# Experts' weights laid down by partition and loaded by 2 MB, in a ring of nine 16-KB tiles

## The chip, the cores and the metric

The program runs on one core of a Trainium2 chip. The metric is the device time of one execution in microseconds. Three executions of the kernel before were timed: 2105.32, 2105.45 and 2109.12 us, median 2105.45 us.

## What is computed

Three blocks follow each other on one sequence of 256 tokens with 1024 features, all in float32. The change lies in the first block's mixture of experts, cut here to what matters:

```python
probs = softmax(h2 @ w_router + b_router)
vals, idx = lax.top_k(swapaxes(probs, 1, 2), cap)      # 16 experts, each takes 32 tokens
for each expert e:
    xe = h2[idx[e]]                                    # [32, 1024]
    ye = (silu(xe @ w_gate_e[e]) * (xe @ w_up_e[e])) @ w_down_e[e]
    out[idx[e]] += vals[e] * ye
```

`w_gate_e` and `w_up_e` are [16, 1024, 2048], `w_down_e` is [16, 2048, 1024]: 8 MB for each of an expert's three matrices, 24 MB for an expert, 384 MB in all (MB is 1,048,576 bytes where loads are counted). Each weight is used once, for 32 tokens.

## The kernel before

`body` (L1667) runs `block1`, `moe`, `block2`, and twice `mixers` and `ffn`. All weights come in by `Net.load` (L71), on SP's queue, in the order in which they are written down. `Net.slot` (L79) hands out the tiles of a ring in turn; a tile is [128, 2048] floats, 8 KB per partition. `load_rows` (L85) cuts a weight into loads of up to 2048 columns per partition, 1 MB each. A row of the weight is a contiguous run in DRAM: a gate or up load is [128, 2048], one run of 8 KB per partition; a down load is [128, 2, 1024], two runs of 4 KB; a load of [128, 4, 512] has four runs of 2 KB.

The ring is six tiles (L41); in block 1 five more are added (L1673). `moe` goes on with these eleven, and puts the six row tiles of block 1's pool `ap8` in where they come free (L701): 17 tiles, 17 MB. From block 2 on it is the six tiles again (L1682). A load into a tile waits until the last reader of the tile's former content is done. SP also waits, at each load, for the landing of the load eight before it (the semaphores `DMAHW0` to `DMAHW7` in the order of the instructions), so at most eight are on their way.

In `moe` (L692) an expert's `gate` and `up` are eight loads each: per load eight matmul instructions of PE at L814, four column groups side by side. Then `hs = silu(gate) * up` on ACT and DVE (L827, L828), its transposes on PE (L831, L839), and eight loads of `down` with their matmuls at L857. The result is scaled on DVE (`Y`, L860) and scattered back to tokens by PE (L864). The first expert's matmuls stand between those that gather the chosen rows (`gather`, L756).

The last expert's `down` goes by two column halves (L846), in loads of [128, 4, 512]. Behind the first half, `out(0)` (L775) adds the result to `x`, transposes it into block 2's input and squares it; `next_load` (L795) brings the first weights of block 2 and splits them into two ring tiles, and `next_products` (L799) puts their products among the matmuls of the second half.

In block 1, 2 and 3 a projection takes each 1-MB load as pieces that ACT and DVE split in two (L99, L100) and PE multiplies three times (L147, L148, L149).

Of the kernel before, what the change touches and what calls it, by code (L numbers as in the profile page):

```python
# [9 lines left out]
F32 = mybir.dt.float32  # L10
# [16 lines left out]
RING_A8 = (6, 7, 8, 9, 12, 15)  # L27


def row_bc(src, n):  # L30
    """A [n] DRAM vector seen by all partitions."""
    return bass.AP(src.tensor, src.offset, [[0, P], [1, n]])


class Net:
    def __init__(self, ctx, tc, a, vo, out):
# [4 lines left out]
        self.rings = [(pool("wrp", 6), "wr")] * 6  # L41
        self.ring_at, self.last_load, self.last_mm = 0, None, None
# [21 lines left out]
    def hT(self, tag, dt=F32R):  # L64
        """One of the two [128, 8, 256] tiles that carry a phase's transposed input."""
        return self.hp.tile([P, 2048], dt, tag=tag, name=tag).rearrange("p (k t) -> p k t", t=S)
# [4 lines left out]
    def load(self, dst, src):  # L71
        """The loads on this queue go out in the order that they are written down in."""
# [6 lines left out]
    def slot(self, dt=F32):  # L79
        """The next tile of the loads' rings."""  # L80
        pool, tag = self.rings[self.ring_at % len(self.rings)]
        self.ring_at += 1
        return pool.tile([P, 2064 if tag == "a8" else 2048], dt, tag=tag, name="wr")

    def load_rows(self, src):  # L85
        """The rows of src [k * 128, n] as [128, k tiles, n], in loads of up to 2048 columns; yields (first k tile, view)."""
# [15 lines left out]
    def behind(self, ins):  # L102
        """The next weights that are split wait on DVE behind ins."""
        self.held = [ins] * 3

    def split_to(self, t, raw):
        """Weights split into the two halves of a tile."""
# [15 lines left out]
    def proj(self, xh, xl, loads, n, evac, ahead=0):  # L123
        """out[half][128, n] = sum over k; loads are (first k tile, raw view [128, k tiles, n]). The first half of the rows
        takes the last pieces, ahead in number, before the second one does."""
# [27 lines left out]
    def queued(self):  # L153
        """The products of this block go out behind the last one that was noted, whichever is ready first."""
# [3 lines left out]
    def table(self, func, after):  # L158
        """Has the activation function's table in place before the data is; after [128, 1] is the last user of another one."""
        self.nc.scalar.activation(self.cp.tile([P, 1], F32, tag="warm", name="warm"), after, func)  # L160

    # Side work goes between the pieces of the projections: generators, run a step at a time in order.
# [4 lines left out]
    def soon(self, f):  # L167
        """Ahead of the other side work: one such closure per step."""
# [8 lines left out]
    def step(self):  # L177
        """A step of the first task, and of the next ones while the steps are light."""
# [7 lines left out]
    def finish(self, gen=None):  # L186
        """Emits side work up to the end of gen, or all of it."""
# [5 lines left out]
    def proj_cols(self, xh, xl, w, c0, n, evac, ahead=0):  # L193
        """Column chunk [c0, c0 + n) of a weight."""
# [9 lines left out]
    def rstd(self, ms, n, d, name, pool=True):  # L204
        """(ms / d + eps) ** -0.5 on [128, n] sums of squares: a power on Pool, or Newton steps on DVE where Pool is busy."""
# [11 lines left out]
        # Newton steps r (3 - t r r) / 2, with the factors -1/2 put off to the end  # L217
# [7 lines left out]
    def sumsq(self, x, n, name, ss=None):  # L225
        """Sums of squares over the last axis of x [128, 2, n], into ss [128, 2]."""
# [7 lines left out]
    def transpose_to(self, src, kts, consume, k0=0):  # L234
        """src [128 tok, 2, kts * 128] -> consume(kt, n, bank [128, n, 256]) for pairs of kt from k0 on."""
# [29 lines left out]
    def input_T(self, gain, name):  # L265
        """The residual stream as the next phase's input: its rows' rstd, and x^T * gain split in two, by column
        halves as they come. The rows' rstd is applied to the products, not to x."""
# [12 lines left out]
class InputT:  # L280
# [6 lines left out]
    def columns(self, c, soon=False):  # L287
        """Column half c; soon: its transposes go between the next projection's pieces."""
# [18 lines left out]
def gate_row(N, dst, src, j0, off):  # L307
    """dst[p, :] = mod[off:off + 1024] for every p, from column tiles j0, j0 + 1 of src, plus b_ada."""
# [10 lines left out]
def block1(N, stop):  # L319
    nc, a, tc = N.nc, N.a, N.tc  # L320
    x = N.x
    with ExitStack() as ctx:
# [3 lines left out]
        p8 = ctx.enter_context(tc.tile_pool(name="ap81", bufs=1))  # L326
# [1465 lines left out]
```

## Time and profile before

| | |
|---|---|
| median of the runs | 2105.45 us |
| runs | 2105.32 to 2109.12 us |
| span of the profiled execution | 2108.0 us (first to last instruction) |
| PE busy | 1756.7 us, 83% |
| DVE / ACT / POOL busy | 819.4 / 603.7 / 181.9 us |
| moved by DMA | 616.02 MB, mean 292 GB/s |

The profile takes one execution apart; that execution's time outside the profiler isn't given, so its span, 2108.0 us, stands for it, 2.6 us above the median of the runs. The page cuts the span into 40 slices of 52.7 us: busy tenths of each engine, TensorE's granted clock in tenths, the busy share of the 16 DMA engines in tenths, and what they moved. The experts lie between about 264 and 1198 us, slices 6 to 22. The chain of waits follows the work that ended last back to the start.

### The profile page before, as it was taken

Reading aid. Unit: us, or ns where it says so; the run is one execution under the profiler, and the core shown is the slowest. Engines: PE = TensorE matmul, PEld = TensorE weight load, DVE = VectorE, ACT = ScalarE, POOL = GpSimd, SP = SyncE. Lnnn points to the kernel's source line nnn. Section 1 sums busy time; section 2 is a strip of 40 time slices with the busy share of each in tenths; the row PEclk is TensorE's granted clock in tenths of the full one; section 3 lists DMA queues with packets and bytes.
Section 4 is the critical chain, followed back from the end, with each engine's and each line's share of the span. In section 5 each row is a group of like instructions: output and inputs, shape, how many; then the busy total and the mean of one; then the engine's idle time right before and its main releaser. Section 6 shows DMA issues by size and latency. Waiting matters only on the chain.

```text
span 2108.0 us, 22814 instructions
## 1 busy us (share of the span) xinstructions
PE 1756.7 (83%) x8895; PEld 1002.8 (48%) x8895; DVE 819.4 (39%) x1563; ACT 603.7 (29%) x1074; POOL 181.9 (9%) x135
## 2 busy tenths in 40 slices
PE   7989786566666666666666899999999999999998
PEld 4767631110110111111100487777778888778886
DVE  4797610000000000000000356676775545786554
ACT  4545410000000000000000345445545445455443
POOL 0671100000000000000000131112010000110000
PEclk9999897877777777766777899999999999999999
DMA  9879699999999999999999773336325556516551
GB/s 363 351 287 348 242 386 422 422 423 422 421 424 424 421 422 423 422 423 420 424 424 423 281 275 120 130 124 210 123 94 183 180 180 207 162 52 198 193 171 70
DMA packets 174396, 616.02 MB, mean 292 GB/s; under 512 B 11336, under 2 KB 20744, under 8 KB 139216
## 3 DMA queue, kind: packets, MB, share of 16 engines
q1 hardware_dynamic: 170288, 601.21, 73.4%
q0 software_dynamic: 3568, 12.75, 1.9%
q8 instruction: 70, 1.15, 0.2%
q10 hardware_dynamic: 432, 0.60, 0.1%
q14 instruction: 38, 0.31, 0.0%
HBM read 613.45 MB, written 4.24 MB: 293 GB/s over the span
## 4 chain that ended last, share of the span: by engine, by line
PE 51%; DMA 41%; DVE 5%; ACT 1%; issue 1%; POOL 0%; POOLq 0%; SPq 0%; DVEq 0%; ACTq 0%
DMA wr<-w_gate_e_dram 14%; DMA wr<-w_up_e_dram 14%; PE pb L147 13%; PE pb L148 13%; PE pb L149 13%; DMA wr<-w_down_e_dram 13%; PE pb L814 2%; DVE wl L100 2%; PE pb L242 2%; PE pb L1360 2%; PE pb L1372 1%; PE po L1398 1%; PE pb L760 1%; PE pb L1056 0%; PE pb L1055 0%
## 5 line engine op out<-in xcount | busy, mean ns | idle before, releaser
L100 DVE TENSOR_TENSOR wl<-wr,wh 128x1024 fp32r<-128x1024 f32 (+1 forms) x380 | 416.3, 1106 | 259.5 <-ACT wh L99 258.8
L814 PE MATMUL pb<-wr,XT 128*32 128x512 f32 x2048 | 362.8, 801 | 183.2 <-DMA wr<-w_up_e_dram 108.6
L99 ACT CAST wh<-wr 128x1024 fp32r<-128x1024 f32 (+1 forms) x380 | 340.0, 897 | 337.0 <-PE pb L149 313.1
L147 PE MATMUL pb<-wh,hh 128*128 128x512 f32 (+3 forms) x992 | 392.2, 396 | 1.8 <-ACT wh L99 1.2
L148 PE MATMUL pb<-wl,hh 128*128 128x512 f32 (+3 forms) x992 | 379.7, 383 | 6.6 <-DVE wl L100 6.5
L149 PE MATMUL pb<-wh,hl 128*128 128x512 f32 (+3 forms) x992 | 379.3, 383 | 0.0
L814 PEld LDWEIGHTS pb<-wr,XT 128*32 128x32 f32 x2048 | 47.9, 122 | 480.7 <-DMA wr<-w_up_e_dram 273.9
L857 PE MATMUL pb<-wr,hT 128*32 128x512 f32 x1024 | 186.7, 807 | 90.4 <-DMA wr<-w_down_e_dram 82.9
L828 DVE TENSOR_TENSOR hs<-pb,hs 128x512 f32<-128x512 f32 x16 | 11.1, 692 | 573.7 <-PE pb L814 573.7
L147 PEld LDWEIGHTS pb<-wh,hh 128*128 128x128 f32 x992 | 189.7, 191 | 50.0 <-issue 12.7
L148 PEld LDWEIGHTS pb<-wl,hh 128*128 128x128 f32 x992 | 189.8, 191 | 43.4 <-DVE wl L100 11.3
L149 PEld LDWEIGHTS pb<-wh,hl 128*128 128x128 f32 x992 | 189.3, 191 | 34.7
L827 ACT ACTIVATE hs<-pb 128x512 f32<-128x512 f32 x16 | 9.6, 598 | 543.9 <-PE pb L814 543.9
L857 PEld LDWEIGHTS pb<-wr,hT 128*32 128x32 f32 x1024 | 30.4, 127 | 229.3 <-DMA wr<-w_down_e_dram 194.6
L860 DVE TENSOR_TENSOR Y<-pb,gfr 128x512 f32<-128x512 f32 (+1 forms) x17 | 11.8, 692 | 269.1 <-PE pb L857 269.1
L841 ACT COPY Sc<-pb 128x256 f32<-128x256 f32 x16 | 6.0, 373 | 324.8 <-PE pb L839 324.8
L788 POOL TENSOR_TENSOR x<-x,grow 128x512 f32<-128x512 f32 x4 | 5.1, 1285 | 913.0 <-ACT jk L231 913.0
L147 PE MATMUL pb<-wh,ah 128*128 128x512 f32 x176 | 69.9, 397 | 0.0
L148 PE MATMUL pb<-wl,ah 128*128 128x512 f32 x176 | 69.6, 395 | 0.0
L149 PE MATMUL pb<-wh,al 128*128 128x512 f32 x176 | 69.6, 395 | 0.0
L864 PE MATMUL acc<-Y,Sc 64*128 64x512 f32 x128 | 45.9, 813 | 15.3 <-DVE Y L860 15.3
L1353 ACT ACTIVATE sb<-sb,cm 128x256 f32<-128x256 f32 x64 | 32.1, 503 | 40.5 <-DVE cm L1350 40.5
(505 smaller groups left out, 1794.3 us busy)
## 6 DMA issues: line engine op xcount, KB each, us to landing
wr<-w_gate_e_dram SPq DMA_DIRECT2D x128, 1024.0 KB, 19.6
wr<-w_up_e_dram SPq DMA_DIRECT2D x128, 1024.0 KB, 19.7
wr<-w_down_e_dram SPq DMA_DIRECT2D x128, 1024.0 KB, 19.6
wr<-w_in_dram SPq DMA_DIRECT2D x62, 1024.0 KB, 7.9
wr<-w_ada_dram SPq DMA_DIRECT2D x24, 1024.0 KB, 12.2
wr<-w_gate_dram SPq DMA_DIRECT2D x22, 1024.0 KB, 5.1
wr<-w_up_dram SPq DMA_DIRECT2D x22, 1024.0 KB, 5.1
wr<-w_down_dram SPq DMA_DIRECT2D x20, 1024.0 KB, 5.0
```

Of the source, the lines that this page charges most:

```text
L99: self.nc.scalar.copy(hi, src)
L100: self.nc.vector.tensor_tensor(lo, src, hi.bitcast(F32), ALU.subtract)
L147: nc.tensor.matmul(o, xh[:, kt, tok], hv[:, k, :], start=kt == first, stop=False)
L148: nc.tensor.matmul(o, xh[:, kt, tok], lv[:, k, :], start=False, stop=False)
L149: self.last_mm = nc.tensor.matmul(o, xl[:, kt, tok], hv[:, k, :], start=False, stop=kt == last).ins
L242: self.nc.tensor.transpose(pv[:, j, h * P:(h + 1) * P], src[:, h, (k + j) * P:(k + j + 1) * P], self.ident)
L760: nc.tensor.matmul(pg, part[:, h, k * P:(k + 1) * P], G[:, h, es].rearrange("p e c -> p (e c)"), start=(h == 0 and i == 0), stop=(h == 1 a ...
L814: N.last_mm = nc.tensor.matmul(pacc[32 * j:32 * j + 32, :], XT[:, k + kk, e, :], wt[:, kk, j * 512:(j + 1) * 512], start=(k + kk == 0), st ...
L857: nc.tensor.matmul(py[32 * q:32 * q + 32, :], hT[:, b, 32 * j:32 * j + 32], wt[:, i, n * 512 - c0:n * 512 - c0 + 512], start=(j == 0 and b ...
L864: nc.tensor.matmul(acc[n][h], Sc[r, h * P:(h + 1) * P], Y[r, :], start=(e == 0), stop=(e == NE - 1))
L1353: nc.scalar.activation(sb[:, c], (ps if bias is None else sb)[:, c], AF.Exp, bias=mm[:, h:h + 1], accum_out=sm[:, h:h + 1])
L1360: nc.tensor.matmul(ps[:, h * S:(h + 1) * S], q[:, h * P:(h + 1) * P], k, start=True, stop=True, tile_position=tile_position)
```

## The change

- The three experts' weights are laid down on the host as [16 experts, 4 loads, 128, 4096]: `we_gate`, `we_up` and `we_down`. Each load is then one contiguous 2 MB in DRAM, with one run of 16 KB for each partition. The last expert's `we_down` is laid down by column halves.
- `load_packed` loads these into whole 16-KB tiles. Of the last expert's second half, the second 2 MB come as two loads of 1 MB.
- The ring's tiles are [128, 4096], 16 KB: three, three more in block 1, and three more in `moe` from a new pool `wx2`, which lies where `ap8` lay (`ap8` now ends with block 1). All other loads stay 1 MB and take the two halves of a tile one after the other; the tile comes free when both are used.
- The scratch for descriptors that POOL writes is 4 KB per partition (`SCRATCH`) and was 16 KB by default.
- `rxT`, the router's transposed rows, moves from `ap8` to the tile `b8`. Comments and docstrings are gone.

```diff
-RING_A8 = (6, 7, 8, 9, 12, 15)
+SCRATCH = 4096
...
-        self.rings = [(pool("wrp", 6), "wr")] * 6
-        self.ring_at, self.last_load, self.last_mm = 0, None, None
+        self.rings = [(pool("wrp", 3), "wr")] * 3
+        self.ring_at, self.rest, self.last_load, self.last_mm = 0, None, None, None
...
-    def slot(self, dt=F32):
-        """The next tile of the loads' rings."""
+    def slot(self, dt=F32, wide=False):
+        if self.rest is not None and not wide:
+            t, self.rest = self.rest, None
+            return t
         pool, tag = self.rings[self.ring_at % len(self.rings)]
         self.ring_at += 1
-        return pool.tile([P, 2064 if tag == "a8" else 2048], dt, tag=tag, name="wr")
+        t = pool.tile([P, 4096], dt, tag=tag, name="wr")
+        self.rest = None if wide else t[:, 2048:]
+        return t if wide else t[:, :2048]
+
+    def load_packed(self, src, n, narrow=()):
+        at = 0
+        for i in range(src.shape[0]):
+            for q in ((0, 2048), (2048, 4096)) if i in narrow else ((0, 4096),):
+                m = q[1] - q[0]
+                t = self.slot(wide=m == 4096)
+                self.load(t, src[i, :, q[0]:q[1]])
+                yield at, t.rearrange("p (a b) -> p a b", b=n)
+                at += m // n
...
-            self.xT = N.T("rxT", F32, 4)
+            self.xT = N.b8("rxT").rearrange("p h n -> p (h n)")[:, :1024].rearrange("p (k t) -> p k t", t=S)
...
+        wx2 = ctx.enter_context(tc.tile_pool(name="wx2", bufs=3))
...
-        for i in RING_A8:
-            N.rings.insert(i, (N.ap8, "a8"))
+        for i in (4, 5, 8):
+            N.rings.insert(i, (wx2, "wr"))
...
-            N.ahead += [(k, p, N.split_to(N.slot(F32R), p)) for k, p in N.pieces(raw, at)]
+            t = N.slot(F32R, wide=True)
+            N.ahead += [(k, p, N.split_to(t[:, 2048 * i:2048 * i + 2048], p)) for i, (k, p) in enumerate(N.pieces(raw, at))]
...
-            for w, pacc in ((a["w_gate_e"], psG), (a["w_up_e"], psU)):
+            for w, pacc in ((a["we_gate"], psG), (a["we_up"], psU)):
...
-                for k, wt in N.load_rows(w[0, e]):
+                for k, wt in N.load_packed(w[e], 2048):
...
-                for at, wt in N.load_rows(a["w_down_e"][0, e, :, c0:c0 + 512 * len(ns)]):
-                    if c0 and at == 4:
-                        next_products()
+                wd = a["we_down"][e]
+                for at, wt in N.load_packed(wd if len(ns) > 1 else wd[2 * ns[0]:2 * ns[0] + 2], 512 * len(ns), (1,) if c0 else ()):
                     for i in range(wt.shape[1]):
+                        if c0 and at + i == 4:
+                            next_products()
...
-        with tc.tile_pool(name="bm", bufs=1) as N.bm, tc.tile_pool(name="wx1", bufs=5) as wx, \
-                tc.tile_pool(name="ap8", bufs=6) as N.ap8:
-            N.rings = N.rings + [(wx, "wr")] * 5
+        N.rings0 = N.rings
+        with tc.tile_pool(name="bm", bufs=1) as N.bm, tc.tile_pool(name="wx1", bufs=3) as wx:
+            N.rings = N.rings + [(wx, "wr")] * 3
             N.router = Router(N)
-            block1(N, stop)
+            with tc.tile_pool(name="ap8", bufs=6) as N.ap8:
+                block1(N, stop)
...
-        N.rings, N.ring_at = [r for r in N.rings if r[0] not in (wx, N.ap8)], 0
+        N.rings, N.ring_at, N.rest = N.rings0, 0, None
...
+def experts(inputs):
+    r = {}
+    for n, name in (("we_gate", "w_gate_e"), ("we_up", "w_up_e")):
+        w = np.asarray(inputs[name])[0]
+        r[n] = np.ascontiguousarray(w.reshape(NE, 4, 2, P, 2048).transpose(0, 1, 3, 2, 4)).reshape(NE, 4, P, 4096)
+    w = np.asarray(inputs["w_down_e"])[0]
+    d = np.ascontiguousarray(w.reshape(NE, 4, 4, P, D).transpose(0, 1, 3, 2, 4)).reshape(NE, 4, P, 4096)
+    d[-1] = w[-1].reshape(2, 8, P, 2, 512).transpose(3, 0, 2, 1, 4).reshape(4, P, 4096)
+    r["we_down"] = d
+    return r
...
-    nc = bacc.Bacc("TRN2", target_bir_lowering=False, num_devices=1)
+    nc = bacc.Bacc("TRN2", target_bir_lowering=False, num_devices=1, dynamic_dma_scratch_size=SCRATCH)
```

What moves on the engines: the compute instructions of PE, DVE, ACT and POOL stay the same in number and, but for about a dozen that change places by a few at the start and at the end of the experts, in order. SP's loads of the experts become half as many and twice as large. At the last expert's three matrices and the loads behind them, SP's order before is (`wr` are tiles of the ring, `128x4x512` is partitions x runs x columns):

```order
L73 DMA wr<-w_gate_e_dram 128x2048 x8
L73 DMA wr<-w_up_e_dram 128x2048 x8
L73 DMA wr<-w_down_e_dram 128x4x512 x4
L73 DMA wr<-w_in_dram 128x4x512
L73 DMA wr<-w_down_e_dram 128x4x512 x4
L73 DMA wr<-w_in_dram 128x4x512
L73 DMA wr<-w_in_dram 128x4x280 x2
```

And in the changed kernel:

```order
L73 DMA wr<-we_gate_dram 128x4096 x4
L73 DMA wr<-we_up_dram 128x4096 x4
L73 DMA wr<-we_down_dram 128x4096 x2
L73 DMA wr<-w_in_dram 128x4x512
L73 DMA wr<-we_down_dram 128x4096
L73 DMA wr<-we_down_dram 128x2048 x2
L73 DMA wr<-w_in_dram 128x4x512
L73 DMA wr<-w_in_dram 128x4x280 x2
```

The bytes come in the same order; the first column half of `down`, four loads of 1 MB, is now two of 2 MB.

In block 2, where the ring is six halves, SP's order before has a wait for a tile at every load (`DMAHW` are the landings, `DVE` is the tile's last split):

```order
L73 DMA wr<-w_in_dram 128x4x512 [waits DMAHW0_49,DVE_49]
L73 DMA wr<-w_in_dram 128x4x512 [waits DMAHW1_49,DVE_49]
L73 DMA wr<-w_in_dram 128x4x512 [waits DMAHW2_49,DVE_49]
L73 DMA wr<-w_in_dram 128x4x512 [waits DMAHW3_49,DVE_49]
L73 DMA wr<-w_in_dram 128x4x512 [waits DMAHW6_49,DMAHW4_49,DVE_49]
```

And in the changed kernel at every second one:

```order
L73 DMA wr<-w_in_dram 128x4x512 [waits DMAHW2_49,DMAHW1_49,DVE_49]
L73 DMA wr<-w_in_dram 128x4x512
L73 DMA wr<-w_in_dram 128x4x512 [waits DMAHW4_49,DMAHW3_49,DVE_49]
L73 DMA wr<-w_in_dram 128x4x512
L73 DMA wr<-w_in_dram 128x4x512 [waits DMAHW5_49,DMAHW7_49,DMAHW0_49,DVE_49]
```

A pair of loads now waits for both halves of its tile, and its second load for nothing more.

## Rows read from the trace of the kernel before

**Rows 1.** The page's 40 slices: busy tenths, granted clock, DMA share, GB/s.
```profile
PE   7989786566666666666666899999999999999998
PEclk9999897877777777766777899999999999999999
DMA  9879699999999999999999773336325556516551
GB/s 363 351 287 348 242 386 422 422 423 422 421 424 424 421 422 423 422 423 420 424 424 423 281 275 120 130 124 210 123 94 183 180 180 207 162 52 198 193 171 70
```

**Rows 2.** The page's chain that ended last, by engine and by line.
```profile
PE 51%; DMA 41%; DVE 5%; ACT 1%; issue 1%; POOL 0%; POOLq 0%; SPq 0%; DVEq 0%; ACTq 0%
DMA wr<-w_gate_e_dram 14%; DMA wr<-w_up_e_dram 14%; PE pb L147 13%; PE pb L148 13%; PE pb L149 13%; DMA wr<-w_down_e_dram 13%; PE pb L814 2%; DVE wl L100 2%; PE pb L242 2%; PE pb L1360 2%; PE pb L1372 1%; PE po L1398 1%; PE pb L760 1%; PE pb L1056 0%; PE pb L1055 0%
```

**Rows 3.** SP's waits (us in total, times, longest), and DMA issues (KB each, us to landing).
```profile
SPq L73 <- DMA wr<-w_gate_e_dram: 247.1, 120, 2.9
...
wr<-w_gate_e_dram SPq DMA_DIRECT2D x128, 1024.0 KB, 19.6
...
wr<-w_gate_dram SPq DMA_DIRECT2D x22, 1024.0 KB, 5.1
```

**Rows 4.** The chain in order of time through three experts: start us, us, what.
```profile
348.44 19.75 DMA wr<-w_gate_e_dram
...
368.26 19.55 DMA wr<-w_up_e_dram
...
387.86 1.11 PE pb L814 x8
...
389.83 18.24 DMA wr<-w_down_e_dram
...
408.14 19.53 DMA wr<-w_gate_e_dram
...
506.91 1.96 PE pb L814 x8
508.87 19.36 DMA wr<-w_down_e_dram
...
528.29 19.69 DMA wr<-w_gate_e_dram
...
1126.11 19.58 DMA wr<-w_gate_e_dram
```

**Rows 5.** Windows: busy us (x instructions) of PE, PEld, DVE, ACT, POOL; PEclk, DMA, GB/s.
```profile
20.00:45.00 25.00, 23.79 (x116) 14.67 (x116) 14.03 (x28) 11.96 (x22) 2.62 (x2) 0.86 1.06 395
...
197.00:203.00 6.00, 6.00 (x29) 4.75 (x28) 5.25 (x12) 5.25 (x9) 0.00 (x0) 1.00 1.07 388
...
348.50:368.20 19.70, 13.00 (x72) 2.26 (x72) 0.69 (x1) 0.00 (x0) 0.00 (x0) 0.80 1.01 425
```

**Rows 6.** The page's count of DMA packets by size.
```profile
DMA packets 174396, 616.02 MB, mean 292 GB/s; under 512 B 11336, under 2 KB 20744, under 8 KB 139216
```

**Rows 7.** PE in order of time, last expert and an earlier one: start, us, idle before.
```profile
1040.39 1.94 PE L814 MATMUL pb<-wr,XT 128*32 128x512 f32 x8 [0.54 <-DMA wr<-w_up_e_dram]
...
1072.56 1.06 PE L814 MATMUL pb<-wr,XT 128*32 128x512 f32 x8 [0.90 <-DMA wr<-w_gate_e_dram]
...
1170.34 8.03 PE L857 MATMUL pb<-wr,hT 128*32 128x512 f32 x32 [0.40 <-issue]
1187.34 1.91 PE L857 MATMUL pb<-wr,hT 128*32 128x512 f32 x8
```

**Rows 8.** SP in order of time at the first experts' loads: start us, us, load.
```profile
265.88 0.38 SPq L73 DMA_DIRECT2D wr<-w_down_e_dram  x1
...
268.46 0.37 SPq L73 DMA_DIRECT2D wr<-w_down_e_dram  x1
```

**Rows 9.** Windows of block 1 and of block 3, columns as in rows 5.
```profile
50.00:100.00 50.00, 50.00 (x209) 38.58 (x208) 37.50 (x40) 24.28 (x42) 29.33 (x14) 1.00 0.88 346
...
1700.00:1800.00 100.00, 100.00 (x488) 83.24 (x487) 55.47 (x90) 51.02 (x77) 5.94 (x10) 1.00 0.61 200
```

More of the change, by code (lines that the diff above doesn't have):

```diff
@@ L326, in block1 @@
         p8 = ctx.enter_context(tc.tile_pool(name="ap81", bufs=1))
+        N.b8 = b8
         N.m2 = ctx.enter_context(tc.tile_pool(name="m21", bufs=4))
@@ L1759 @@
 _RAW = ["x", "w_ada", "b_ada", "w_in", "b_gate", "w_fourier", "w_conv_out", "w_o", "w_router", "b_router",
-        "w_gate_e", "w_up_e", "w_down_e", "g_final", "w_in_2", "cmp_w1_k_2", "cmp_w1_v_2", "cmp_w2_k_2", "cmp_w2_v_2",
+        "g_final", "w_in_2", "cmp_w1_k_2", "cmp_w1_v_2", "cmp_w2_k_2", "cmp_w2_v_2",
         "w_branch_a_2", "w_branch_b_2", "w_o_2", "norm_post_2",
         "w_in_3", "diff_lambda_3", "w_uq_3", "w_ukv_3", "t5_table_3", "w_o_3", "w_gate_3", "w_up_3", "w_down_3", "final_norm_3"]
+def experts(inputs):
[8 more added lines that the diff above has]
+    return r
 def arrays_of(inputs):
@@ L1767, in arrays_of @@
     arrays["vecs"], vo = pack(inputs)
+    arrays.update(experts(inputs))
     for c in "kv":
```

## The prediction

> **What bounds the kernel now.** I read the page's slices first, then the chain, then the experts alone. In the slices [rows 1] the kernel has two parts: in slices 7 to 21 the DMA engines are full (9 tenths throughout, 420 to 424 GB/s) and PE stands at 5 or 6 tenths, with a granted clock of 0.6 to 0.7; elsewhere PE has 8 or 9 tenths and the DMA share drops, behind the experts to 3 to 6 tenths. The chain says the same [rows 2]: 41% of the span is the three experts' weights, and the rest is mostly PE's products at L147 to L149. So a change to the experts' loads is worth what it does to the DMA engines' rate between 264 and 1198 us, and a change to the ring is worth something elsewhere only if PE comes to wait for a load.
>
> Inside the experts nothing but the rate counts. SP's waits at L73 are ended by landings, 2.9 us at the longest [rows 3], which is about one load's time: a load goes out when an earlier one is in. The stretch of one gate matrix has DMA 1.01, 425 GB/s, and PE busy for 13.00 of 19.70 us [rows 5]. PE works off a 1-MB load in 1.06 us or in 1.94 us, about the ratio of the clock's two levels (2.4 and 1.2 GHz), and then waits for the next landing [rows 7].
>
> The chain in order of time gives the three rates [rows 4]. Gate, runs of 8 KB: 368.26 − 348.44 = 19.82 us. Up, the same form: 387.86 − 368.26 = 19.60. I take their mean, 19.71 us for 8 MB. Down, runs of 4 KB: 408.14 − 387.86 = 20.28 us. Thirteen experts, from 348.44 to 1126.11, take 777.67 us, 59.82 each, so that a down takes 59.82 − 2 × 19.71 = 20.40 us on the mean. The mean hides two kinds of down: 528.29 − 506.91 = 21.38 us is one of three long downs among the thirteen; the other ten take (13 × 20.40 − 3 × 21.38) / 10 = 20.11. The 2-KB runs at the kernel's start move 395 GB/s with DMA full [rows 5]. The shorter the run, the slower: there is a cost for each run beside that of its bytes.
>
> **The cost of a 16-KB run.** An engine moves a sixteenth of 8 MB, 512 KB: 64 runs of 8 KB or 128 of 4 KB. That is 19.71 / 64 = 308.0 ns and 20.11 / 128 = 157.1 ns. A straight line through both has 308.0 − 157.1 = 150.9 ns for 4 KB and 6.2 ns for the run. A 16-KB run would take 6.2 + 4 × 150.9 = 609.8 ns, and 32 of them 19.51 us. Through the mean of all downs (159.4 ns) the line gives 10.8 ns a run, and 19.37 us. I take 19.50 us, since the long downs come at wide intervals and need not hang on run length. What the line can't show is whether it holds beyond 8 KB: that is an extrapolation by a factor of two. Its ends are kept for the range: 19.37 us from one side, and no gain over 8-KB runs, 19.71 us, from the other; worse than that is a rival below.
>
> **The sum.**
> - Gate and up: 15 of the 16 experts have both matrices wholly in the DMA-bound stretch (the first gate and up are loaded ahead while block 1 ends), 30 × (19.71 − 19.50) = −6.3 us.
> - Down: 15 matrices less the part that is loaded ahead, 14.9 × (20.11 − 19.50) = −9.1 us. For the three long downs I take the same 0.6 us, as if their extra 1.3 us stayed.
> - The last expert's first half, 4 MB, is in 2-KB runs: 4.194 MB at 395 GB/s are 10.62 us, and half of 19.50 is 9.75: −0.9 us.
> - Behind it: PE begins on the last load of this half when it has landed. That load now carries 16 matmuls at L857 and had 8, which take 1.91 us [rows 7]. `Y`, the scatter and block 2's input come behind them: +1.9 us, and no more of it is won back, since PE is busy from there to the end of the experts. Should PE's longer wait there bring the clock down, sixteen would take about four times that, 7.6 us, so the upper bound is +5.7; the lower bound is 0, if the stretch is held by DVE's split of the next weights instead.
> - The start: the ring is full when the first matmuls begin, and the next load goes out at 265.88, when the first tile is free; the second comes at 268.46 [rows 8]. The wide tile is free only when both its k tiles are used, so it goes out some 2.6 us later. But 18 MB instead of 17 are in by then, and 1 MB is 19.71 / 8 = 2.5 us of loading. I take 0, with −1 and +1 as bounds.
> - PE per load: two k tiles at the low clock take 2 × 1.94 = 3.9 us, under the 4.9 us that 2 MB take to land. The cover holds. If it were gone, the experts would cost 3.9 us for each 2 MB and still not more than the landings.
> - The ring in block 1: DMA stands at 0.88 and PE is busy for 50.00 of 50.00 us [rows 9]. A pair of loads waits for a tile whose halves were loaded twelve and eleven loads before; one load of the old ring waited for the one eleven before. 0, within 1 us either way.
> - The ring in blocks 2 and 3: six halves as before, but the first load of a pair goes out one use later, so four loads instead of five lie between. A load lands 5.1 us after its issue [rows 3]; at 200 GB/s [rows 9] four 1-MB loads are 21 us of PE's work. PE is at 100.00 of 100.00 us there. 0. If that cover were gone, PE would wait up to 5.1 us at a pair.
> - The 4-KB scratch, `rxT` in `b8`, the compute order: the same instructions, and none with a new wait that lies late. 0.
>
> −6.3 − 9.1 − 0.9 + 1.9 = −14.4 us. The sum is made against the profiled execution, 2108.0 us, which stands 2.6 us above the median; the difference carries over to the median: 2105.45 − 14.4 = **2091 us**. With 19.37 us a matrix, the long downs like the others (3 × 1.3 us) and 0 for the tail it is 30 × 0.34 + 14.9 × 0.74 + 3.9 + 1 = 26 us, 2079.
>
> **Rivals.**
>
> *The rate stays.* The engines, or what feeds them, are at their best at 8-KB runs, or a 16-KB run is cut in two on the way: the change doesn't do what it says. 8-KB runs are not cut today: of 174,396 packets 139,216 are under 8 KB [rows 6], so 35,180 are of 8 KB or more, and the experts' gates and ups alone have 256 loads × 128 = 32,768 runs of 8 KB. Gate and up then give 0, down 14.9 × (20.11 − 19.71) = −6.0, the last half −0.8, the tail +1.9: −4.9 us, 2101. For it: the gain from 4 to 8 KB is already down to 2%. Against it: a cost for each run shows at three lengths, and nothing in the rows flattens.
>
> The Trainium skill, "DMA: Bandwidth & Descriptors", gives 425 GB/s for the largest transfer in its table "Measured (HBM→SBUF, 128 partitions, SWDGE, issued from GpSimd)". That is the number of this trace's gate stretch, and by it this rival would hold. The same page's section "Where 436 GB/s comes from" sets 435.2 GB/s as the ceiling, which leaves 2.4% above that stretch; no row shows more than 425. An estimate from that ceiling is 8.389 MB / 435.2 GB/s = 19.28 us a matrix, at which the time would be about 2081.
>
> *Longer runs are slower.* The trace moves runs over 8 KB only once, in block 1's scan, where POOL's queue carries `t5d<-t5v` beside weights: the window around it has 388 GB/s with DMA full [rows 5]. If 16-KB runs went at that, because one engine held by a long run keeps the others' ends of the load waiting, a matrix would take 8.389 MB / 388 GB/s = 21.62 us, and the kernel would be 30 × 1.91 + 14.9 × 1.51 + 0.2 + 1.9 = 82 us slower, 2187. It decides from 19.81 us a matrix on: there gate and up lose 30 × 0.10 = 3.0, down wins 14.9 × 0.30 = 4.5, the last half wins 0.7 and the tail loses 1.9, all about zero. Against it: that transfer goes from DRAM to DRAM and shares the engines with 2-KB and 4-KB runs, so the window is the mix's rate and not the run's.
>
> *The tail grows.* The tail's +1.9 could reach +5.7 and the start +1; the sum would then be −9.6, 2096. That is a part of the likeliest case and has no chance of its own.
>
> **How the numbers follow.** A measurement of this kernel tells 0.2%, 4.2 us, from no change. The likeliest case, the line holds, has 0.78; its own range is 2083 to 2098. The upper end has 19.60 us a matrix and +4 us in the tail: 30 × 0.11 + 14.9 × 0.51 + 0.8 − 4.0 = 7.7. The plateau has 0.13, at 2101, of which half falls within 0.2%; longer runs slower has 0.09, any size up to +82. So faster by over 0.2% has 0.78 + 0.06 = 0.84, within 0.2% 0.07, slower 0.09. The range goes from 2083, since the full 26 us would need all good bounds together, to the plateau's 2101.
>
> **What the profile of the change would show.** If the line holds: the chain's pieces of gate, up and down are all about 19.5 us, an expert 58.5 instead of 59.8, and the experts' slices have 429 to 430 GB/s; loads land 39 us after issue; packets under 8 KB are fewer by 34,816 (15 downs of 8 × 256 runs of 4 KB, the last one's 8 × 512 of 2 KB); PE in 1700 to 1800 us is still at 100%; at the end of the last expert's first half L857 runs 16 matmuls behind the last landing. If gate and up keep 19.6 to 19.8 us and only down falls to it, the plateau was right. If an expert takes over 59.8 us, or SP's waits at L73 are ended by PE instead of landings, I am wrong.

## The result, and the profile after

| | changed | before |
|---|---|---|
| median of the runs, us | 2096.64 (4 runs, 2092.09 to 2098.11) | 2107.28 (4 runs, 2105.32 to 2111.33) |
| ratio to before | 0.9947 (95%: 0.9930 to 0.9964) | |
| span of the profiled execution, us | 2095.7 | 2108.0 |
| DMA packets, of them under 8 KB | 128456, 101344 | 174396, 139216 |

The kernel is 10.6 us faster by the medians, a ratio that lies clear of the 0.2% that separates it from no change. The forecast was 14.4 us less and 2091 us, in a range from 2083 to 2101. A second comparison with before gave 0.9957 (0.9940 to 0.9974).

The slices of the changed kernel's page (busy tenths of PE, granted clock, DMA share, GB/s) answer to [rows 1], the packets to [rows 6], the issue row to [rows 3]:

```profile
PE   7989785655655565566556999999999999999998
PEclk9999898788788878887887999999999999999999
DMA  9979699999999999999999753337225546415542
GB/s 366 362 273 376 242 383 430 431 430 432 430 430 431 430 432 431 430 431 430 431 430 431 288 187 121 121 126 229 90 83 199 179 176 215 160 46 201 183 169 91
DMA packets 128456, 615.97 MB, mean 294 GB/s; under 512 B 8280, under 2 KB 17688, under 8 KB 101344
...
wr<-we_gate_dram SPq DMA_DIRECT2D x64, 2048.0 KB, 38.8
```

One window in the middle of the experts, before and then changed (columns as in [rows 5]):

```profile
600.00:780.00 180.00, 118.40 (x626) 19.69 (x626) 7.76 (x15) 2.91 (x6) 0.00 (x0) 0.74 1.02 423
```

```profile
600.00:780.00 180.00, 105.71 (x644) 23.59 (x640) 7.76 (x15) 3.50 (x7) 0.00 (x0) 0.82 1.01 431
```

The experts' slices have 430 to 432 GB/s and had 420 to 424. DMA is as full as before, so the engines move more in the same busy time. The packets under 8 KB fell by 37,872. That is the 34,816 of the downs, as forecast, and 3056 under 512 B, 16 for each of the 191 loads fewer (587 and 396 on SP's queue). A load lands 38.8 us after its issue.

The chain in order of time (start us, us, what) answers to [rows 4]. A piece is now one load from issue to landing, with eight loads of 2 MB on their way, so it stands for 16 MB or two matrices:

```profile
403.10 38.83 DMA wr<-we_up_dram
441.99 38.84 DMA wr<-we_gate_dram
480.89 38.83 DMA wr<-we_down_dram
519.79 40.53 DMA wr<-we_up_dram
560.38 38.67 DMA wr<-we_gate_dram
```

From piece to piece it is 441.99 − 403.10 = 38.89 us, 19.45 us a matrix, alike for gate, up and down. 19.50 was forecast, and 19.71 and 20.11 stood before. A piece of 40.53 us is what was the long down before: the extra 1.7 us stayed, as assumed. Over thirteen experts, from landing to landing, an expert takes 58.63 us instead of 59.81.

The gain ends with the experts. Where the last expert's scatter begins, the chain of the kernel before and the PE timeline of the changed one have:

```profile
1198.99 2.00 PE acc L864 x4
```

```profile
1151.56 8.76 PE L878 MATMUL pb<-wr,hT 128*32 128x512 f32 x32 [1.28 <-DMA wr<-we_down_dram]
...
1181.13 1.98 PE L885 MATMUL acc<-Y,Sc 64*128 64x512 f32 x4 [0.80 <-DVE Y L881]
```

There the changed kernel is 17.9 us ahead, and at the end 12.4 (the spans before rounding). The start times of the same PE instruction in both traces share it out:

| part | change, us | forecast, us |
|---|---|---|
| block 1 and the start of the experts (what is left of the 17.9) | −1.1 | 0 |
| 15 experts, 59.81 to 58.63 us each | −17.7 | −15.4 |
| last expert's first half, 10.41 to 9.73 us of landings | −0.7 | −0.9 |
| its tail: last landing to PE's end, 2.43 to 4.03 us | +1.6 | +1.9 |
| blocks 2 and 3, behind the experts | +5.5 | 0 |

So the experts gave what was forecast and somewhat more, and something took 5.5 us back in blocks that the forecast put at 0. That, and where the rate comes from, is what the runs are for.

### The profile page after: what moved, and what is told of

Same layout as the page of the kernel before. It is cut to its first block, busy times and chain, and to the rows that moved or that the text cites. A ratio compares the mean times of both kernels' runs of the same rounds, so it can differ in the third digit from the quotient of the medians.

```text
span 2095.7 us, 22337 instructions
## 1 busy us (share of the span) xinstructions
PE 1690.7 (81%) x8895; PEld 1015.5 (48%) x8895; DVE 815.5 (39%) x1563; ACT 602.4 (29%) x1074; POOL 182.5 (9%) x135
## 2 busy tenths in 40 slices
DMA packets 128456, 615.97 MB, mean 294 GB/s; under 512 B 8280, under 2 KB 17688, under 8 KB 101344
## 4 chain that ended last, share of the span: by engine, by line
PE 51%; DMA 42%; DVE 4%; issue 1%; ACT 1%; POOL 1%; SPq 0%; POOLq 0%; ACTq 0%; DVEq 0%
DMA wr<-we_up_dram 14%; PE pb L164 13%; DMA wr<-we_down_dram 13%; DMA wr<-we_gate_dram 13%; PE pb L165 13%; PE pb L166 13%; PE pb L1381 2%; PE pb L259 2%; DVE wl L117 1%; PE pb L878 1%; PE pb L834 1%; PE pb L1393 1%; PE po L1419 1%; DMA wr<-w_fourier_dram 1%; PE pb L779 1%
## 5 line engine op out<-in xcount | busy, mean ns | idle before, releaser
L834 PE MATMUL pb<-wr,XT 128*32 128x512 f32 x2048 | 329.3, 772 | 226.6 <-DMA wr<-we_up_dram 135.7
L834 PEld LDWEIGHTS pb<-wr,XT 128*32 128x32 f32 x2048 | 62.2, 125 | 472.6 <-DMA wr<-we_up_dram 212.4
L878 PE MATMUL pb<-wr,hT 128*32 128x512 f32 x1024 | 165.6, 747 | 96.3 <-DMA wr<-we_down_dram 88.5
L878 PEld LDWEIGHTS pb<-wr,hT 128*32 128x32 f32 x1024 | 35.0, 125 | 210.9 <-DMA wr<-we_down_dram 136.5
L885 PE MATMUL acc<-Y,Sc 64*128 64x512 f32 x128 | 39.1, 700 | 15.2 <-DVE Y L881 15.2
## 6 DMA issues: line engine op xcount, KB each, us to landing
wr<-we_gate_dram SPq DMA_DIRECT2D x64, 2048.0 KB, 38.8
wr<-we_up_dram SPq DMA_DIRECT2D x64, 2048.0 KB, 38.8
wr<-we_down_dram SPq DMA_DIRECT2D x63, 2048.0 KB, 38.8
```

The lines of the kernel that those rows point to most:

```text
L834: N.last_mm = nc.tensor.matmul(pacc[32 * j:32 * j + 32, :], XT[:, k + kk, e, :], wt[:, kk, j * 512:(j + 1) * 512], start=(k + kk == 0), st ...
L878: nc.tensor.matmul(py[32 * q:32 * q + 32, :], hT[:, b, 32 * j:32 * j + 32], wt[:, i, n * 512 - c0:n * 512 - c0 + 512], start=(j == 0 and b ...
L885: nc.tensor.matmul(acc[n][h], Sc[r, h * P:(h + 1) * P], Y[r, :], start=(e == 0), stop=(e == NE - 1))
```

## The experiments

The theories, by the letters that the expectations use. On the rate, **A**: the length of a run sets it. **B**: the size of a load, or the bytes on their way. **A2**: a price for each load beside that for each run. **G**: the address of the tile in SBUF, against **H**: the tile's place in the ring. On half loads, **E**: a load to one half of the partitions has half of the ways in, against **F**: a load of 64 runs is slow as such. On blocks 2 and 3, **C**: the wait of the pairs, against **D**: scatter.

All runs leave the computation as it is. The table has the DMA rate (windows view, 600 to 780 us) and the time of an expert, from landing to landing over thirteen of them. Matrix times in the text are medians over 14 or 15 matrices, worked out from the landings in the trace in the same way. Each rate and expert time is from the one profile that a kernel has.

| kernel | load, run | off tiles | GB/s | expert, us | median, us | ratio to before (95%) |
|---|---|---|---|---|---|---|
| before | 1 MB, 8 and 4 KB | 10 of 17 | 423 | 59.81 | | |
| b_scratch | 1 MB, 8 and 4 KB | 10 of 17 | 423 | 59.81 | 2110.43 | 1.0018 (1.0004 to 1.0032) |
| down8 | 1 MB, 8 KB | 10 of 17 | 425 | 59.39 | 2100.44 | 0.9974 (0.9962 to 0.9986) |
| b_align | 1 MB, 8 and 4 KB | none | 425 | 59.46 | 2103.81 | 0.9989 (0.9978 to 0.9999) |
| b_best | 1 MB, 8 KB | none | 427 | 59.16 | 2100.46 | 0.9972 (0.9959 to 0.9984) |
| two1 | 1 MB, 8 KB | 3 of 9 | 427 | 59.20 | 2101.68 (one run) | |
| run8 | 2 MB, 8 KB | 3 of 9 | 427 | 59.12 | 2106.39 | 0.9994 (0.9981 to 1.0007) |
| alt64 | 1 MB, 16 KB | 3 of 9 | 430 | 58.72 | 2101.41 (one run) | |
| changed (again) | 2 MB, 16 KB | 3 of 9 | 431 | 58.65 | 2099.41 | 0.9957 (0.9940 to 0.9974) |
| half | 2 MB, 16 KB | 3 of 9 | 431 | 58.68 | 2095.55 | 0.9945 (0.9923 to 0.9967) |
| half_tail | 2 MB, 16 KB | 3 of 9 | 430 | 58.67 | 2095.15 | 0.9936 (0.9917 to 0.9955) |
| a_best | 2 MB, 16 KB | none | 431 | 58.66 | 2099.00 | 0.9963 (0.9950 to 0.9977) |

"Off tiles" are those whose address is no multiple of 256 B; more on them below. Kernels that ran together share their runs of before, whose medians were 2106.0 to 2108.7 us.

### Run length against load size

**down8**, the kernel before with packed downs alone (`wd` is the expert's [8, 128, 2048], or a half of it):

```diff
-                for at, wt in N.load_rows(a["w_down_e"][0, e, :, c0:c0 + 512 * len(ns)]):
+                for at, wt in N.load_packed(wd, 512 * len(ns)):
```

> The kernel before with one edit: the downs' weights are laid down so that a load of 1 MB is one run of 8 KB per partition (the last expert's by column halves); ring, load size and gate and up as before. Theory A (the length of a run sets the rate): a down takes what a gate or an up takes, 19.7 us typically instead of 20.0 to 20.1; 14.9 x 0.4 to 0.6 us and 0.9 us for the last half give -7 to -10 us, so 2097 to 2100 us against 2107, and the other blocks do not move. Theory B (the size of a load, or the bytes on their way, sets the rate): loads are still 1 MB, eight on their way, so 2107 us, no change.

A down takes 19.83 us and took 20.19, an expert 59.39 instead of 59.81. The time fell by 5.7 us, a little under theory A's 7 to 10. B, which has no change, is out.

**run8**, the changed kernel's 2-MB loads in two runs of 8 KB:

```diff
-                self.load(t, src[i, :, q[0]:q[1]])
+                self.load(t.rearrange("p (h n) -> p h n", n=2048), src[i, q[0] // 2048:q[1] // 2048].rearrange("h p n -> p h n"))
```

> The changed kernel with its loads of 2 MB in two runs of 8 KB per partition (the host lays each 2 MB down as two blocks of [128, 2048]); tiles, ring and number of loads as changed. Theory A (run length): a matrix goes from 19.45 us typically to 19.73, 45 x 0.28 = +13 us, so 2109 to 2110 us, and 422 to 426 GB/s in the experts. Theory B (load size, bytes on their way): as the changed kernel, 2097 us, 430 GB/s.

An expert takes 59.12 us, half a microsecond more than the changed kernel, and the kernel is as fast as before (0.9994). A has the direction, but the matrix is 19.62 to 19.69 us and not 19.73. Something else in the changed kernel had already helped. Only the run's length differs between run8 and the changed kernel: 59.12 − 58.63 = 0.49 us over 96 runs fewer on each of the 16 DMA engines, 5.1 ns a run.

**two1**, the same with two loads of 1 MB for each tile:

```diff
-                self.load(t, src[i, :, q[0]:q[1]])
+                for c in range(0, m, 2048):
+                    self.load(t[:, c:c + 2048], src[i, :, q[0] + c:q[0] + c + 2048])
```

> The changed kernel with each 16-KB tile filled by two loads of 1 MB on 128 partitions, runs of 8 KB. The kernel with 2-MB loads in runs of 8 KB had 428 GB/s, 19.60 us a matrix, between 19.73 and 19.45. Theory A2 (there is a price for each load beside that for each run): back to 425 GB/s and 19.73 us. Theory A (only the run's length counts, the ring does the rest): 427 to 428 GB/s, 19.60 us.

427 GB/s and 59.20 us, against 59.12: there is next to no price for a load, so A2 is out. Loads of 1 MB in runs of 8 KB are thus faster into this ring than into the old one (down8, 59.39). That left the tiles themselves.

**load1 and alt64**, 1-MB loads in runs of 16 KB, to 64 partitions each. load1 takes the lower and the upper half, alt64 the even and the odd partitions:

```diff
-                self.load(t, src[i, :, q[0]:q[1]])
+                for p in ((0, 64), (64, P)) if m == 4096 else ((0, P),):
+                    self.load(t[p[0]:p[1]], src[i, p[0]:p[1], q[0]:q[1]])
```

```diff
-                self.load(t, src[i, :, q[0]:q[1]])
+                for p in (slice(0, P, 2), slice(1, P, 2)) if m == 4096 else (slice(0, P),):
+                    self.load(t[p], src[i, p, q[0]:q[1]])
```

> The changed kernel with each 16-KB tile filled by two loads of 1 MB, 64 partitions each, in runs of 16 KB; eight loads, 8 MB, are on their way instead of 16 MB. Theory A (run length): a matrix stays at 19.45 us, 2097 us. Theory B (load size or bytes on their way): back to 19.7 us, 2107 to 2110 us.

> The kernel with two loads of 1 MB on 64 partitions each, but every second partition instead of the lower and the upper half. Theory E (a load that writes only one half of the partitions has half of the ways into the tile, which is why that kernel went at 216 GB/s): 425 to 431 GB/s, and the time 2095 to 2110 us; the rate then also tells what 1-MB loads in 16-KB runs are worth, 19.45 us if only the run counts, 19.6 if the load counts too. Theory F (64 runs in a load, or 16-KB runs in pairs of loads, are slow however they lie): 2400 to 2850 us again.

load1 took 2791.86 us (2422.21 to 2842.94 in six runs) and said nothing on A and B: its halves of the partitions set another limit. Its GB/s in the page's slices and, below, the window from 600 to 700 us of alt64 (columns as in [rows 5]):

```profile
GB/s 360 331 293 234 245 250 267 252 291 324 387 245 218 219 220 226 224 222 223 216 216 216 213 216 216 219 167 238 120 120 190 112 150 180 164 230 65 191 190 98
```

```profile
600.00:700.00 100.00, 57.44 (x356) 13.91 (x348) 4.48 (x9) 1.94 (x4) 0.00 (x0) 0.81 1.01 430
```

In load1 the DMA share is 9 tenths from slice 4 to slice 26, and yet 213 to 226 GB/s are moved in slices 13 to 26, over 985 us, and 234 to 387 in the experts' slices ahead of them. So a full busy share doesn't say that the engines move at their full rate. With every second partition the same number of runs of the same length goes at 430 GB/s. So E holds and F is out. The Trainium skill says this in "SBUF — State Buffer", "Door 1: The DMA port swizzle": partitions 0 to 63 reach only 8 of 16 ports, some 218 GB/s at best. The trace agrees with its 213 to 226 of slices 13 to 26. The 387 of slice 11 lie above that, so loads of both halves must have run side by side there. That even partitions alone go at full rate agrees with the table there, in which the port does not hang on a partition's two lowest bits.

alt64 also answers the question that load1 was to answer: with loads of 1 MB, 8 MB on their way and runs of 16 KB an expert takes 58.72 us, against 58.65 for 2-MB loads. The size of a load is worth under 0.1 us an expert here and in two1; the length of its runs is worth five times that.

### The tile's address

In the kernel before, PE's products follow each landing. These are PE's rows in order of time (start us, us, group, idle before):

```profile
1023.09 1.06 PE L814 MATMUL pb<-wr,XT 128*32 128x512 f32 x8 [0.68 <-DMA wr<-w_gate_e_dram]
1025.52 1.94 PE L814 MATMUL pb<-wr,XT 128*32 128x512 f32 x8 [1.37 <-DMA wr<-w_gate_e_dram]
1027.97 1.54 PE L814 MATMUL pb<-wr,XT 128*32 128x512 f32 x8 [0.51 <-DMA wr<-w_up_e_dram]
1030.45 1.06 PE L814 MATMUL pb<-wr,XT 128*32 128x512 f32 x8 [0.94 <-DMA wr<-w_up_e_dram]
1032.94 1.07 PE L814 MATMUL pb<-wr,XT 128*32 128x512 f32 x8 [1.43 <-DMA wr<-w_up_e_dram]
1035.43 1.62 PE L814 MATMUL pb<-wr,XT 128*32 128x512 f32 x8 [1.42 <-DMA wr<-w_up_e_dram]
1037.92 1.94 PE L814 MATMUL pb<-wr,XT 128*32 128x512 f32 x8 [0.86 <-DMA wr<-w_up_e_dram]
```

The steps are 2.43 and 2.45 us, and then four times 2.48 to 2.49. The first two loads went to tiles of `wx1` at 112128 and 136704 B, multiples of 256. The next went to 153152 (`ap8`), 60992, 28224 and 69184 (`wrp`), all 64 B off. It is so over the whole trace: the medians of the gate and up landings, tile by tile, are 2.430 to 2.442 us for the seven tiles at multiples of 256, and 2.473 to 2.488 for the ten others. For downs they are 2.437 to 2.474 and 2.512 to 2.560. In the changed kernel the three `wrp` tiles lie off (4.885 us for 2 MB) and the other six do not (4.848).

**b_align**, the loads and weights of before, all 17 tiles at multiples of 256 B. **b_best** adds the downs of down8:

```diff
+        self.cp.tile([P, 48], F32, name="pad")
...
+            N.bm.tile([P, 16], F32, name="pad2")
...
-        return self.ap8.tile([P, 2064], dt, tag="a8", name=name)
+        return self.ap8.tile([P, 2112], dt, tag="a8", name=name)[:, :2064]
```

> The kernel before, loads and weights untouched; two small pads (192 B and 64 B per partition) and row tiles of 8448 B instead of 8256 put all 17 tiles of the experts' ring at addresses that are multiples of 256 B; room for it comes from the 4-KB scratch. Theory G (a run into a tile at another address takes 5 to 6 ns longer: in the kernel before 10 of 17 tiles lie so, and their 1-MB landings stand 2.48 us apart instead of 2.435 for runs of 8 KB, 2.55 instead of 2.46 for 4 KB): 240 x 10/17 x 0.047 + 120 x 10/17 x 0.09 = 13 us less, 2094 us against 2107, 428 to 430 GB/s. Theory H (the place in the ring, not the address): 2107 us.

> The same aligned ring of 1-MB tiles, and the downs laid down in runs of 8 KB. Theory G: every landing 2.435 us after the last, an expert 58.4 us and what the instruction fetches add; 13 us, 120 x 0.025 = 3 us and 0.9 us for the last half less than before: 2090 us, below the changed kernel, with no wide tile at all. If only the run's length counts (theory A): as the kernel with 8-KB downs, 2100 us.

G holds, with less than half of the size. The two kinds of landings are gone (2.424 to 2.458 us for gate and up on all 17 tiles), and an expert takes 59.46 us instead of 59.81: 15 × 0.35 = 5.3 us of 13. The landings on tiles that lay well before got slower, 2.445 instead of 2.438, and the downs' stand at 2.48 instead of 2.455. So the price taken from the difference of the two kinds was too high; one reading is that part of the short steps before had been the other half of the long ones, which no run tests. The time fell by only 2.2 us, since this kernel pays for its scratch (below). With both edits an expert takes 59.16 us.

The Trainium skill, "DMA: Bandwidth & Descriptors", "How a descriptor splits into AXI transactions", says that a run which does not start at a multiple of 256 B begins with one more, partly unused transaction. The traces agree in direction. The page tells it of what a transaction reads, while the address here is on the written side, and it gives no time for it. All tiles that lie off in these kernels lie off by 64 B, so other distances were not measured.

### Blocks 2 and 3

**half**: in blocks 2 and 3 the halves of three held tiles in turn, so that each load waits for its own half. **half_tail** also splits the last load of the first half:

```diff
+        if self.held_tiles is not None:
+            t = self.held_tiles[self.ring_at % 6 // 2][:, self.ring_at % 2 * 2048:][:, :2048]
+            self.ring_at += 1
+            return t
...
+        N.held_tiles = [N.rings0[0][0].tile([P, 4096], F32, tag="wr", name="wr") for _ in range(3)]
```

```diff
-                for at, wt in N.load_packed(wd if len(ns) > 1 else wd[2 * ns[0]:2 * ns[0] + 2], 512 * len(ns), (1,) if c0 else ()):
+                for at, wt in N.load_packed(wd if len(ns) > 1 else wd[2 * ns[0]:2 * ns[0] + 2], 512 * len(ns), (1,) if len(ns) == 1 else ()):
```

> The changed kernel, and in blocks 2 and 3 the three 16-KB tiles are held and their halves used in turn, so that a load waits for its own half as in the kernel before. Theory C (in blocks 2 and 3 the first load of a pair comes too late, which cost 5.5 us in the changed kernel's profile, at 1440, 1469, 1504, 1803 and 1870 us): these places close up and the time falls by 5 to 6 us to 2091. Theory D (that was the scatter of one execution): 2097 us, and gaps of such a size come at these or other places again.

> The changed kernel again, beside the next one on the same chip. Theory C (the pairs' wait in blocks 2 and 3 costs about 4 us: from 1176 us of the kernel before to the end its profile needs 930.4 us, with loads in 2 x 8 KB 932.0, the one that waits by halves 926.2, the one with 8-KB downs 921.0, the kernel before 924.7): 930 to 932 us again from that instruction on, and 4 to 6 us above the next kernel. Theory D (scatter): the rest lies anywhere between 921 and 932, and the two kernels do not differ by more than the tail's 1.6 us.

> The changed kernel with the halves of the three tiles used in turn in blocks 2 and 3, and the last 2 MB of the last expert's first half as two loads of 1 MB, so that eight matmuls stand behind its last landing and not sixteen. Theory C: 2097 - 4 - 1.6 = 2091 us, and the experts' end 1.6 us nearer to the last landing than in the changed kernel. Theory D: 2095 to 2097 us.

The split of the last load did half of what was expected. In half_tail PE ends the first column half 3.2 us behind its last landing, 0.8 us nearer than in the changed kernel and not 1.6: PE now takes the half's 32 matmuls in 7.06 us without a pause, and starts them only when the transposed `hs` is there, 1.0 us behind the half's first landing.

Neither C nor D holds as put. From 1215 us of the kernel before to the end the profiles lose 5.4 us against it in the changed kernel, 2.1 in its second run, 0.9 in half and 3.3 in half_tail: scatter, whichever way the ring waits. But one place, in the first layer of block 3, comes back again and again. From 1474 to 1498 us of the kernel before, the changed kernel falls back by 2.6 us, and half by 2.5, though there the last load of `w_in` ahead of `w_o` landed at 1452.47 us and not, as in the changed kernel, at 1467.59. So it is not the pairs. down8 does not fall back there (0.1 us). What the others share is the 4-KB scratch.

**b_scratch** is the kernel before with that alone:

```diff
-    nc = bacc.Bacc("TRN2", target_bir_lowering=False, num_devices=1)
+    nc = bacc.Bacc("TRN2", target_bir_lowering=False, num_devices=1, dynamic_dma_scratch_size=4096)
```

> The kernel before with the 4-KB scratch alone. Its descriptors are few (3568 packets on that queue): no change, 2107 us. Everything moves 12,288 B down, a multiple of 256, so theory G expects none either.

It falls back by 2.2 us at that place, and b_best, on the old ring of 1-MB tiles, by 2.6. POOL's timeline at that place (start us, us, what, idle before) of before, b_scratch and the changed kernel, and behind the last one PE's pause in it:

```profile
1468.56 3.29 POOL L1313 DMA_DIRECT2D nb<-rpbd  x4 [17.43 <-PE pb L1489]
...
1476.02 4.59 POOL L1315 TENSOR_TENSOR nb<-nb,nmask 128x2048 f32<-128x2048 f32 x1 [2.66 <-DMA nb<-rpbd]
```

```profile
1467.71 2.49 POOL L1313 DMA_DIRECT2D nb<-rpbd  x3 [18.49 <-PE pb L1489]
1471.62 0.83 POOL L1313 DMA_DIRECT2D nb<-rpbd  x1 [1.42 <-issue]
...
1478.61 4.58 POOL L1315 TENSOR_TENSOR nb<-nb,nmask 128x2048 f32<-128x2048 f32 x1 [4.65 <-DMA nb<-rpbd]
```

```profile
1451.11 2.49 POOL L1334 DMA_DIRECT2D nb<-rpbd  x3 [18.72 <-PE pb L1510]
1455.19 0.83 POOL L1334 DMA_DIRECT2D nb<-rpbd  x1 [1.60 <-issue]
...
1462.37 4.58 POOL L1336 TENSOR_TENSOR nb<-nb,nmask 128x2048 f32<-128x2048 f32 x1 [4.84 <-DMA nb<-rpbd]
```

```profile
1469.56 0.80 PE L164 MATMUL pb<-wh,hh 128*128 128x512 f32 x1 [2.59 <-ACT sb L1374]
```

Before, POOL issues four transfers of `nb` without a gap. With 4 KB it stops for 1.4 to 1.6 us ahead of the fourth, for nothing that the timeline names, and `nb`'s sum starts 10.9 and 11.3 us after the first of them instead of 7.5. The stop comes ahead of the same transfer in all eleven kernels with the small scratch of the table, in both layers of block 3 (1.4 to 2.1 us at the first, 1.4 to 4.8 at the second), and in neither with 16 KB, before and down8. PE falls back by 2.2 to 2.8 us in nine of the eleven, those in which the fourth `nb` also lands 6.8 to 7.8 us after its issue; in b_align and in the changed kernel's second run it lands after 4.1 and 4.3 us, and PE loses nothing. What ends the stop can be read from the landings: in all 22 places the fourth transfer goes out 0.33 us after the first of the four has landed, be that 3.5 or 7.0 us after its issue, while with 16 KB it goes out 1.2 to 1.5 us before that landing. So with the small scratch the fourth transfer waits for the first to land. That the landing gives back room for descriptors is the obvious reading, but the traces show the wait and not what the scratch holds.

At the second layer (1815 to 1830 us) the kernel before itself loses 2.1 us against down8, for a cause that stays open, so it is no measure there. Against down8, six of the eleven, with the sum 10.5 to 12.3 us after the first issue, lose 1.7 to 3.0 us (the changed kernel 2.4), alt64 with 9.8 us loses 1.1, and four with 7.9 to 8.7 us lose 0.2.

In time b_scratch is 0.18% (0.04 to 0.32%) slower than before, about 4 us, and its runs scatter more (2103.12 to 2120.37 us). Its own profile is a favourable one, 3.8 us shorter than that of before, since that execution was spared a stop of 2.8 us near 1540 us which the profile of before has.

**a_best**: half_tail with both pads.

> The changed kernel with both pads (all nine tiles at multiples of 256 B), the tiles used by halves in blocks 2 and 3 and the last 2 MB of the first half in two loads. Theory G: the three tiles that lay off land 4.85 us apart instead of 4.885, 60 x 0.036 = 2.2 us less than the 2095 us of the kernel without the pads: 2093 us. Without G: 2095 us.

The rate did not move (58.66 us an expert against 58.67), and the time is 2099.00 us. The two kinds of landings did go (medians of 4.839 to 4.879 us, tile by tile, for 2 MB), but what that should save, some 0.15 us an expert, doesn't show in the mean of one profile each: landings that come 0.3 us late or more add up to 5.7 us in a_best and to 4.2 in half_tail. So with runs of 16 KB no worth of the address is shown. None of these is clearly better than the changed kernel; half_tail's 0.9936 (0.9917 to 0.9955) overlaps its 0.9957 (0.9940 to 0.9974).

## Why the prediction was right, and where not

**The bound** was right: the stretch is held by the DMA engines, and its rate went from 423 to 431 GB/s. (The clock in slices 7 to 21 of [rows 1] is 0.6 to 0.8, not 0.6 to 0.7; nothing hangs on it.) PE, which was to work off two k tiles in less than a landing, did so: SP's loads still wait for landings, and at the lower clock level sixteen matmuls took 4.0 us, where a landing takes 4.85.

**The 16-KB run.** The forecast drew a line through 8-KB and 4-KB runs and got 6.2 ns for each run and 19.51 us a matrix; 19.45 were measured. Two things lay in that price. Between kernels whose tiles all lie well, runs of 4 KB to 8 KB for the downs (b_align to b_best) give 59.46 − 59.16 = 0.30 us over 64 runs fewer on an engine, 4.7 ns a run. From there to runs of 16 KB (a_best) 59.16 − 58.66 = 0.50 us over 3 × 32 fewer, 5.2 ns; run8 and the changed kernel, whose tiles are the same, give 5.1. So the line does hold past 8 KB, with some 5 ns. The rest of the gain in rate, 0.35 us an expert on the old ring (b_align), is the address of the tiles, of which the forecast knew nothing: of the 1.16 us that an expert fell, 0.42 come with longer downs, some 0.25 with better-lying tiles (down8 to two1 and run8: 59.39 to 59.20 and 59.12), and 0.5 with runs of 16 KB. The mechanism was right, and the 30 × 0.21 + 14.9 × 0.61 us, 15.4 in all, became 17.7.

**The tail** was +1.6 us, with +1.9 forecast, by the step that was named: sixteen matmuls behind the last landing. Its upper bound of +5.7 was misread: the 1.91 us for eight matmuls are already a time at the lower of the clock's levels ([rows 7] have 1.94 and 1.06), and sixteen at it took the 4.03 us of the table, not 7.6.

**Block 1 and the start** were put at 0 within 1 us each. The profiles of the kernels with the changed block 1 stand 4.4 us behind to 2.0 us ahead of before at the experts' first products, so its scatter is larger than the bounds. Within that scatter one step has a sign: from the router's last transposes to the softmax's (248 to 253 us of the kernel before) all eight kernels with the changed pools lose 1.6 to 1.8 us, and the four with the old ones 0.0. POOL's rows there (start us, us, what, idle before), before and then changed:

```profile
247.35 0.57 POOL L706 DMA_DIRECT2D iota<-c_iota_dram  x1 [51.53 <-DVE x L586]
250.58 0.74 POOL L212 TENSOR_TENSOR r_r<-r_t,minus_half 128x2 f32<-128x2 f32 x1 [2.65 <-DVE r_t L209]
```

```profile
247.95 0.57 POOL L725 DMA_DIRECT2D iota<-c_iota_dram  x1 [55.47 <-DVE pl L704]
248.54 0.75 POOL L229 TENSOR_TENSOR r_r<-r_t,minus_half 128x2 f32<-128x2 f32 x1
```

Before, the issue of the `iota` load waited for the residual `x` and was over when `r_r`, the rows' factor that the softmax needs, could start. In the changed kernel it waits for the router's sum `pl`. `r_t`, the input of `r_r`, is done at 246.87 us, but `r_r` stands behind `iota` on POOL's queue until 248.54. Which of the moved pools and tiles brought the wait, no run separates.

**The ring in blocks 2 and 3** was put at 0, and the runs do not contradict it: pairs or halves made no difference that stands out of the scatter.

**The scratch, `rxT` and the order** is the term that failed: "the same instructions, and none with a new wait that lies late. 0." Two new waits came. One is that of `iota` above, which costs 1.7 us ahead of the experts. The other stands in no instruction: with the smaller scratch POOL stops until an earlier transfer has landed, and the kernel that has the scratch alone is about 4 us slower (0.8 to 6.7). Without the scratch the changed kernel would stand near −15 us, beside the forecast's −14.4. That sum of two separately measured kernels is an estimate; a changed ring with the scratch of before was not run. In the sum the errors partly cancel, which is luck: the experts gave 2.3 us more than forecast, and two waits that were put at nothing took that back and more.

**The rivals.** That the rate stays at 425 GB/s fell with the 431 and with alt64. Nothing is cut at 8 KB: the packets of 8 KB or more fell from 35,180 to 27,112, as they do when a run of 16 KB is one packet. By the 425 GB/s of the Trainium skill ("DMA: Bandwidth & Descriptors", "Measured (HBM→SBUF, 128 partitions, SWDGE, issued from GpSimd)") that rival would have held; this trace measures 431, between that figure and the ceiling of 435.2 in the same page's "Where 436 GB/s comes from". That longer runs are slower fell too; the transfer from DRAM to DRAM was no guide.

## What to carry to other kernels

In this kernel, with the DMA engines full and runs of 4 to 16 KB, a run cost about 5 ns beside its bytes. Laying weights down by partition takes part of that back, with loads of 1 MB as with loads of 2 MB. With runs of 4 and 8 KB, ring tiles at multiples of 256 B instead of 64 B off were worth as much as that (0.35 us of an expert's 59.81), for pads of 192 and 64 B and row tiles 192 B longer; with runs of 16 KB no gain was measured. Price the memory that a change takes from elsewhere as well: the descriptor scratch and the moved pools looked free in the order of the instructions, and they were not.

## What was not expected

- Two loads to 64 partitions each moved 213 to 226 GB/s for 985 us with all DMA engines busy, when the halves were lower and upper partitions, and 430 GB/s when they were even and odd.
- With the 4-KB scratch, POOL's fourth transfer in a row went out 0.33 us after the first had landed, in 22 of 22 places.
- Landings in one ring came in two kinds, 2.43 and 2.48 us, by the tile's address.
- TensorE's granted clock in the experts rose from 0.74 to 0.82 (600 to 780 us), between its levels of 1.2 and 2.4 GHz, and PE's busy time there fell from 118.4 to 105.7 us, with about as many matmuls (626 and 644 in the window): they now come sixteen at a time with longer pauses. In all kernels that take sixteen at a time it was 0.78 to 0.84 (alt64, which waits for two loads of 1 MB, 0.82), and in those that take eight 0.70 to 0.74 (two1 0.72). It changed nothing in the time, since PE waits for landings there.
